# Attention times V: probabilities as the stationary operand, so that results come out with queries on partitions

## The chip, the cores and the metric

The kernel runs on one core of a Trainium2 chip. The metric is device time in microseconds (us), as the median of several executions. Engines are named as the profile names them: PE is the tensor engine, which multiplies matrices (PEld is its loading of weights, the stationary operand), ACT is ScalarE, which does the exponentials, DVE is VectorE, and SP issues the DMAs.

## The reference

A batch of 32 sequences, 512 positions, 8 heads of 64. For each sequence:

```
q, k, v = split(x_b @ w_qkv)                      # per head: [len, 64]
scores  = (q @ k.T) / sqrt(64)
attn    = exp(scores - max) / sum
out_b   = attn @ v                                # rows beyond len stay zero
```

## The kernel before

The kernel works in float16 with float32 sums, over all 512 positions, and masks by length. Per batch it transposes x (tiles `pxt`, `xT`), projects to q, k (`pq`, `qkT`) and v (`pv`, `v_aug`), computes scores with keys on partitions (`psc`), takes the exponential on ACT (`ep`), and multiplies by V. V carries one more column with the key mask, so the sum of the probabilities (the denominator) comes out of the same product. A compiler orders the instructions of all engines from this source.

Scores and exponentials (not touched by the change). The two heads of a pair use different halves of the array's rows:

```python
            for kt in range(NT):                               # 4 key tiles
                psc = ps_s.tile([P, 2, MAXS], FP32, tag="pssc")    # pool of 2
                for par in range(2):
                    rq = 64 * par
                    nc.tensor.matmul(psc[:, par, :],
                        qkT[rq : rq + 64, NC + i, kt * P : (kt + 1) * P],
                        qkT[rq : rq + 64, i, :], start=True, stop=True)
                nc.scalar.activation(out=ep[:, :, kt, :], in_=psc, func=AF.Exp, scale=scale)
```

The product with V. V is stationary, 512 queries stream, and the result has 65 head columns on partitions and queries along the row:

```python
                pav = ps_a.tile([P, MAXS], FP32, tag="psa")        # pool of 4
                for kt in range(NT):
                    nc.tensor.matmul(pav[0 : HD + 1, :], v_aug[:, kt, h, :],
                        ep[:, par, kt, :], start=(kt == 0), stop=(kt == NT - 1))
                nc.vector.tensor_copy(out=avout[0 : HD + 1, h, :], in_=pav[0 : HD + 1, :])
```

A separate output stage, one batch later, turns it round again with 32 PE transposes (`pot`), and normalises:

```python
        for qt in range(NT):
            pot = ps_a.tile([P, NH, HD + 2], F16, tag="psa")
            for h in range(NH):
                nc.tensor.transpose(pot[:, h, 0 : HD + 1],
                    avout[0 : HD + 1, h, qt * P : (qt + 1) * P], ...)
            # den8 = pot[:, :, HD] + qbig;  rcp8 = 1 / den8
            # out_nat[:, qt, :] = pot[:, :, 0:HD] * rcp8        (8 heads at once)
```

`qbig` is 1e30 for queries beyond the length, so those rows become zero.

The softmax here doesn't subtract the row's maximum and nothing guards it: scores larger than these inputs give would overflow.

## Time and profile before

The median is 948.5 us.

| | before |
|---|---|
| time, median of 4 | 948.5 us (946.9 to 950.4) |
| PE, DVE, ACT busy in the span | 94%, 63%, 58% |
| mean granted PE clock | 0.982 |
| one batch, mean of 20 in the middle of the trace | 28.44 us |

The first lines of the page give busy time, share and number of instructions of each engine; the chain that ended last follows the waits back from the end:

```profile
PE 891.2 (94%) x5120; PEld 363.4 (38%) x5120; DVE 592.6 (63%) x1094; ACT 547.5 (58%) x645; POOL 1.1 (0%) x8
...
PE 83%; ACT 10%; DVE 3%; issue 2%; DMA 1%; POOLq 0%; ACTq 0%; POOL 0%
```

They say "bound by PE". The groups of instructions (line, engine, operation, output <- input, shapes, count; then busy us, mean ns of one, and idle time before it with what ended it) show what the change will remove:

```profile
L180 ACT ACTIVATE ep<-psc 128x1024 f16<-128x1024 f32 x512 | 484.1, 1072 | 355.1 <-PE psc L173 355.1
L197 DVE CAST avout<-pav 65x512 f16<-65x512 f32 x256 | 172.9, 686 | 243.5 <-PE pav L190 243.5
L190 PE MATMUL pav<-ep,v_aug 128*65 128x512 f16 x1024 | 297.0, 388 | 0.0
...
L219 PE MATMUL pot<-ident_f_95,avout 65*128 65x65 f16 x1024 | 45.9, 194 | 2.8 <-DVE out_nat L232 1.4
```

The timeline of one batch (start and length in us, engine, line, what, count, and in brackets the idle time before) shows two stages and a tail:

```profile
301.72 0.60 PE L173 MATMUL psc<-qkT 64*128 64x512 f16 x3
302.14 12.02 ACT L180 ACTIVATE ep<-psc 128x1024 f16<-128x1024 f32 x13 [8.92 <-PE psc L173]
...
310.63 0.39 PE L173 MATMUL psc<-qkT 64*128 64x512 f16 x2
310.95 0.62 PE L190 MATMUL pav<-ep,v_aug 128*65 128x512 f16 x2
311.50 0.39 PE L173 MATMUL psc<-qkT 64*128 64x512 f16 x2
...
312.70 2.10 PE L190 MATMUL pav<-ep,v_aug 128*65 128x512 f16 x8
314.64 0.65 PE L219 MATMUL pot<-ident_f_95,avout 65*128 65x65 f16 x16
...
316.38 1.94 ACT L180 ACTIVATE ep<-psc 128x1024 f16<-128x1024 f32 x2 [2.21 <-PE psc L173]
...
319.70 1.03 PE L128 MATMUL pq<-xT,w_r 128*128 128x512 f16 x4
```

Read it so. ACT had been idle for 8.92 us, while PE did projections; then it does 13 exponentials in a row, 0.91 us apart. In most steps of this row PE does a pair of score matmuls and two products with V. In the tail the last eight products (2.10 us) and the output transposes go by, ACT is idle for 2.21 us, and the next projections (`pq`) start at 319.70. In a pair of score matmuls the second starts 3 to 6 ns after the first: they run side by side.

### The profile page before, as it was taken

How to read it: one execution, taken by the hardware profiler on the slowest of the kernel's cores; microseconds unless marked ns; L12 is line 12 of the kernel's file. 1: busy time of each engine (PE TensorE's matmuls, PEld its weight loads, DVE VectorE, ACT ScalarE, POOL GpSimd, SP SyncE). 2: the span in 40 equal slices, each digit the busy share in tenths (PEclk: the TensorE clock that was granted, in tenths of full speed). 3: DMA queues.
4: the chain of work that ended last, by engine and by line, in shares of the span. 5: the costliest groups of instructions: out<-in, count | busy, mean ns of one | idle time of the engine just before them, and what ended most of it. 6: DMA issues, size and time to landing. Idle time of an engine off the chain costs nothing.

```text
span 945.1 us, 12346 instructions
## 1 busy us (share of the span) xinstructions
PE 891.2 (94%) x5120; PEld 363.4 (38%) x5120; DVE 592.6 (63%) x1094; ACT 547.5 (58%) x645; POOL 1.1 (0%) x8
## 2 busy tenths in 40 slices
PE   2999999999999999999999999999999999999995
PEld 1433434433334433334433334433334433344332
DVE  2745667756667665567756667665566656666555
ACT  3177555576565567455576565567554575645764
POOL 0000000000000000000000000000000000000000
PEclk9899999999999999999999999999999999999997
DMA  9410222220222220222220222220122110111102
GB/s 330 159 45 1 89 89 89 90 72 31 76 90 89 89 89 23 68 90 89 90 72 32 76 89 90 89 82 25 72 90 89 45 45 1 45 45 45 45 26 108
DMA packets 34426, 71.05 MB, mean 75 GB/s; under 512 B 1090, under 2 KB 1090, under 8 KB 34370
## 3 DMA queue, kind: packets, MB, share of 16 engines
q1 hardware_dynamic: 34370, 70.26, 21.2%
q8 instruction: 40, 0.66, 0.3%
q14 instruction: 16, 0.13, 0.0%
HBM read 36.70 MB, written 33.55 MB: 74 GB/s over the span
## 4 chain that ended last, share of the span: by engine, by line
PE 83%; ACT 10%; DVE 3%; issue 2%; DMA 1%; POOLq 0%; ACTq 0%; POOL 0%
PE pav L190 25%; PE pq L128 23%; PE psc L173 18%; PE pv L142 12%; ACT ep L180 8%; PE pxt L118 3%; DVE avout L197 2%; PE pot L219 2%; ACT xT L121 2%; DMA w_f<-in_w_qkv_dram 1%; DVE out_nat L232 0%; ACT w_r L74 0%; POOLq L277 0%; ACTq L180 0%; DVE iota_f L86 0%
## 5 line engine op out<-in xcount | busy, mean ns | idle before, releaser
L180 ACT ACTIVATE ep<-psc 128x1024 f16<-128x1024 f32 x512 | 484.1, 1072 | 355.1 <-PE psc L173 355.1
L197 DVE CAST avout<-pav 65x512 f16<-65x512 f32 x256 | 172.9, 686 | 243.5 <-PE pav L190 243.5
L190 PE MATMUL pav<-ep,v_aug 128*65 128x512 f16 x1024 | 297.0, 388 | 0.0
L128 PE MATMUL pq<-xT,w_r 128*128 128x512 f16 x1024 | 239.5, 388 | 7.3 <-ACT w_r L74 7.2
L173 PE MATMUL psc<-qkT 64*128 64x512 f16 x1024 | 215.5, 385 | 17.0 <-ACT ep L180 13.1
L135 DVE CAST qkT<-pq 128x512 f16<-128x512 f32 x256 | 171.2, 689 | 58.9 <-PE pq L128 57.2
L128 PEld LDWEIGHTS <-w_r 128*128 128x128 f16 x1024 | 98.3, 100 | 128.6 <-issue 16.6
L190 PEld LDWEIGHTS <-v_aug 128*65 128x65 f16 x1024 | 84.2, 110 | 125.7 <-issue 100.1
L173 PEld LDWEIGHTS <-qkT 64*128 64x128 f16 x1024 | 60.5, 93 | 180.3 <-issue 170.9
L142 PE MATMUL pv<-w_r,xT 128*128 128x512 f16 x512 | 115.7, 379 | 0.0
L149 DVE TENSOR_SCALAR v_aug<-pv,kmask 128x512 f16<-128x512 f32 x128 | 96.4, 753 | 16.0 <-PE pv L142 5.5
L121 ACT COPY xT<-pxt 128x512 f16<-128x512 f16 x128 | 70.6, 603 | 22.6 <-PE pxt L118 22.0
L142 PEld LDWEIGHTS <-xT 128*128 128x128 f16 x512 | 50.1, 98 | 60.4
L219 PE MATMUL pot<-ident_f_95,avout 65*128 65x65 f16 x1024 | 45.9, 194 | 2.8 <-DVE out_nat L232 1.4
L219 PEld LDWEIGHTS <-avout 65*128 65x128 f16 x1024 | 38.9, 98 | 19.6 <-issue 7.8
L118 PE MATMUL pxt<-ident_f_95,x_129 128*128 128x128 f16 x16 | 1.9, 308 | 11.7 <-DVE ident_f_95 L67 11.7
L74 ACT CAST w_r<-w_f 128x1536 f16<-128x1536 f32 x4 | 5.8, 1488 | 5.3 <-DMA w_f<-in_w_qkv_dram 5.3
L154 DVE CAST v_aug<-kmask 128x32 f16<-128x32 f32 x32 | 7.4, 230 | 0.0
L118 PEld LDWEIGHTS <-x_129 128*128 128x128 f16 x16 | 1.7, 142 | 11.6 <-DVE x_129 L112 7.4
L112 DVE CAST x_129<-x_nat 128x2048 f16<-128x2048 f32 x1 | 1.2, 1227 | 6.1 <-DMA x_nat<-in_x_dram 6.1
L89 DVE TENSOR_TENSOR kmask<-iota_f,len_f 128x128 f32<-128x128 f32 x1 | 0.3, 292 | 5.1 <-POOL len_f L81 5.1
L86 DVE CAST iota_f<-iota_i 128x4 f32<-128x4 int32 x1 | 0.2, 246 | 3.8 <-POOL iota_i L84 3.8
(490 smaller groups left out, 262.4 us busy)
## 6 DMA issues: line engine op xcount, KB each, us to landing
x_nat<-in_x_dram SPq DMA_DIRECT2D x32, 1024.0 KB, 6.5
out_dram<-out_nat SPq DMA_DIRECT2D x32, 1024.0 KB, 4.9
w_f<-in_w_qkv_dram SPq DMA_DIRECT2D x4, 768.0 KB, 8.9
len_84<-in_lengths_dram SPq DMA_DIRECT2D x1, 0.2 KB
```

Source lines behind the costliest of these rows:

```text
L118: nc.tensor.transpose(pxt[:, t, :], x16[:, t, c * P : (c + 1) * P], ident_f16)
L121: nc.scalar.copy(out=xT[:, c, :], in_=pxt.rearrange("p t q -> p (t q)"))
L128: nc.tensor.matmul(pq, w_r[:, c, m * P : (m + 1) * P], xT[:, c, :], start=(c == 0), stop=(c == NC - 1),)
L135: nc.vector.tensor_copy(out=qkT[:, m, :], in_=pq)
L142: nc.tensor.matmul(pv, xT[:, c, t * P : (t + 1) * P], w_r[:, c, 2 * D : 3 * D], start=(c == 0), stop=(c == NC - 1),)
L149: nc.vector.tensor_scalar_mul(v_aug[:, t, :, 0:HD], pv.rearrange("p (h d) -> p h d", d=HD), kmask[:, t, b : b + 1],)
L154: nc.vector.tensor_copy(out=v_aug[:, :, :, HD], in_=kmask[:, :, b].unsqueeze(2).broadcast_to([P, NT, NH]),)
L173: nc.tensor.matmul(psc[:, par, :], qkT[rq : rq + 64, NC + i, kt * P : (kt + 1) * P], qkT[rq : rq + 64, i, :], start=True, stop=True,)
L180: nc.scalar.activation(out=ep[:, :, kt, :], in_=psc, func=AF.Exp, scale=scale)
L190: nc.tensor.matmul(pav[0 : HD + 1, :], v_aug[:, kt, h, :], ep[:, par, kt, :], start=(kt == 0), stop=(kt == NT - 1),)
L197: nc.vector.tensor_copy(out=avout[0 : HD + 1, h, :], in_=pav[0 : HD + 1, :])
L219: nc.tensor.transpose(pot[:, h, 0 : HD + 1], avout[0 : HD + 1, h, qt * P : (qt + 1) * P], ident_f16[0 : HD + 1, 0 : HD + 1],)
```

## The change

Swap the operands of the product. The probabilities of 128 queries are stationary, V with its ones column (65 columns) streams, and the result has queries on partitions, as the output needs it. The output transposes and the eviction to `avout` go; normalisation follows at once, for two heads and 128 queries at a time.

```diff
-            for par in range(2):
-                h = 2 * i + par
-                pav = ps_a.tile([P, MAXS], FP32, tag="psa")
-                for kt in range(NT):
-                    nc.tensor.matmul(pav[0 : HD + 1, :], v_aug[:, kt, h, :],
-                        ep[:, par, kt, :], start=(kt == 0), stop=(kt == NT - 1))
-                nc.vector.tensor_copy(out=avout[0 : HD + 1, h, :], in_=pav[0 : HD + 1, :])
+            for qt in range(NT):
+                pav = ps_a.tile([P, 2, HD + 1], FP32, tag="psa")
+                for par in range(2):
+                    for kt in range(NT):
+                        nc.tensor.matmul(pav[:, par, :],
+                            ep[:, par, kt, qt * P : (qt + 1) * P],
+                            v_aug[:, kt, 2 * i + par, :],
+                            start=(kt == 0), stop=(kt == NT - 1))
+                # den2 = pav[:, :, HD] + qbig;  rcp2 = 1 / den2
+                # out_nat[:, qt, i * P : (i + 1) * P] = pav[:, :, 0:HD] * rcp2
...
-    def stage_out(b):            # 32 transposes per batch, normalisation of 8 heads
...
-    for i in range(B + 2):
+    for i in range(B + 1):
```

Cuts are marked with dots; calls are drawn together. 1024 large products become 4096 small ones, and 1024 transposes go.

More of the change, by code (lines that the diff above doesn't have):

```diff
@@ L105 @@
     vaug_t = [None] * B
-    avout_t = [None] * B
     def stage_qkv(b):
@@ L161, in stage_attn @@
         v_aug = vaug_t[b]
-        avout = bav.tile([P, NH, MAXS], F16, tag="avout")
-        avout_t[b] = avout
+        out_nat = bo.tile([P, NT, D], FP32, tag="out_nat")
         etp = [None] * (NH // 2)
@@ L185, in emit_av @@
             ep = etp[i]
-            for par in range(2):
-                h = 2 * i + par
-                pav = ps_a.tile([P, MAXS], FP32, tag="psa")
-                for kt in range(NT):
-                    nc.tensor.matmul(
-                        pav[0 : HD + 1, :],
-                        v_aug[:, kt, h, :],
-                        ep[:, par, kt, :],
-                        start=(kt == 0),
-                        stop=(kt == NT - 1),
-                    )
-                nc.vector.tensor_copy(
-                    out=avout[0 : HD + 1, h, :], in_=pav[0 : HD + 1, :]
+            for qt in range(NT):
+                pav = ps_a.tile([P, 2, HD + 1], FP32, tag="psa")
+                for par in range(2):
+                    for kt in range(NT):
+                        nc.tensor.matmul(
+                            pav[:, par, :],
+                            ep[:, par, kt, qt * P : (qt + 1) * P],
+                            v_aug[:, kt, 2 * i + par, :],
+                            start=(kt == 0),
+                            stop=(kt == NT - 1),
+                        )
+                den2 = sml.tile([P, 2], FP32, tag="den2")
+                nc.vector.tensor_scalar(
+                    out=den2,
+                    in0=pav[:, :, HD],
+                    scalar1=qbig[:, qt, b : b + 1],
+                    scalar2=None,
+                    op0=ALU.add,
+                )
+                rcp2 = sml.tile([P, 2], FP32, tag="rcp2")
+                nc.vector.reciprocal(out=rcp2, in_=den2)
+                nc.vector.tensor_tensor(
+                    out=out_nat[:, qt, i * P : (i + 1) * P].rearrange(
+                        "p (h d) -> p h d", d=HD
+                    ),
+                    in0=pav[:, :, 0:HD],
+                    in1=rcp2.unsqueeze(2).broadcast_to([P, 2, HD]),
+                    op=ALU.mult,
                 )
@@ L208, in stage_attn @@
         emit_av(3)
-    def stage_out(b):
-        avout = avout_t[b]
-        avout_t[b] = None
-        out_nat = bo.tile([P, NT, D], FP32, tag="out_nat")
-        for qt in range(NT):
-            den8 = sml.tile([P, NH], FP32, tag="den8")
-            rcp8 = sml.tile([P, NH], FP32, tag="rcp8")
-            pot = ps_a.tile([P, NH, HD + 2], F16, tag="psa")
-            for h in range(NH):
-                nc.tensor.transpose(
-                    pot[:, h, 0 : HD + 1],
-                    avout[0 : HD + 1, h, qt * P : (qt + 1) * P],
-                    ident_f16[0 : HD + 1, 0 : HD + 1],
-                )
-            nc.vector.tensor_scalar(
-                out=den8,
-                in0=pot[:, :, HD],
-                scalar1=qbig[:, qt, b : b + 1],
-                scalar2=None,
-                op0=ALU.add,
-            )
-            nc.vector.reciprocal(out=rcp8, in_=den8)
-            nc.vector.tensor_tensor(
-                out=out_nat[:, qt, :].rearrange("p (h d) -> p h d", d=HD),
-                in0=pot[:, :, 0:HD],
-                in1=rcp8.unsqueeze(2).broadcast_to([P, NH, HD]),
-                op=ALU.mult,
-            )
         nc.sync.dma_start(out=out[b].rearrange("(t p) d -> p t d", p=P), in_=out_nat)
-    for i in range(B + 2):
+    for i in range(B + 1):
         if i < B:
@@ L244 @@
             stage_attn(i - 1)
-        if i >= 2:
-            stage_out(i - 2)
 _INS = ['x', 'w_qkv', 'lengths', 'n_heads']
```

## The prediction

> What bounds it now. The page's busy shares (PE 94%, DVE 63%, ACT 58%) mislead: in the timeline two stages alternate, about 28.2 us per batch (between ends of V projections; mostly 27.6 and 28.9).
> (1) Projection: 48 matmuls of 512 columns, 216 ns start to start, 10.4 us, PE-bound; ACT idle for about 9 us (the waits give ACT 355 us idle, ended by the score matmuls).
> (2) Attention: 12 or 13 exponentials back to back. A row of 13 lasts 12.02 us; less one duration (1.07) over 12 is 0.91 us each. In such a step PE does one score pair and two probability-times-V matmuls (0.32 + 0.56 us) and is full too: a balance of ACT and PE.
> (3) A tail of about 6 us: the last 8 to 10 probability-times-V matmuls (2.1 to 2.5 us), 32 output transposes with score matmuls between, x transposes and copies. ACT is idle 2.2 to 2.7 us there.
>
> Removed: 1024 matmuls of 512 columns (216 to 242 ns apart, about 230 us of PE), 1024 output transposes (16 in 0.65 us, the last 0.19: 31 ns each, about 35 us), 256 evictions of 65x512 (172.9 us of DVE), 128 sets of wide output operations.
> Added: 4096 matmuls with 65 moving columns, each with its own 128-column weights. The output transposes have that shape but for 65 rows instead of 128: 31 ns. The Trainium skill (TensorE: Matmul & The Clock Gate, LDWEIGHTS) says load time goes by columns, not rows; nothing in this trace shows it at 128 rows. Estimate 4096 x 31 ns = 127 us. So PE sheds about 140 us. DVE: 512 sets of add, reciprocal, multiply: pitches 0.13 and 0.12 us, and a multiply over 128 instead of 512 columns, about 0.20 us (its 0.60 us pitch less 384 columns at the 0.96 GHz of the skill's VectorE: DVE Perf Modes). 0.45 us a set, 0.75 if each waits for the one before: 230 to 380 us, against about 310 removed. DVE stays under 80%.
>
> Critical path. The compiled order puts 14 exponentials (12 of this batch, two of the next) in one row behind the projection, with 8 to 12 small matmuls between score pairs: 0.25 to 0.37 us plus 0.32 us per 0.91 us step, so PE has slack and ACT alone paces: 0.4 + 14 x 0.91 = 13.1 us. Four x copies follow (0.47 us each); projections start under them. So 13.1, about 2 us until the last copy, some 9.4 us for the projections left then: 24.5 to 25.3 us per batch instead of 28.2. The row hardly shrinks; the gain is the PE tail (2 us of large matmuls, 1.5 to 2 us of transposes) and ACT's idle in it. 30 periods save about 100 us; at the end there is no separate output stage: 5 to 8 us more.
>
> Predicted 835 us, range 805 to 872. Faster by over 2%: 0.94; within 2%: 0.04; slower: 0.02.
>
> To check: exponentials 0.91 us apart in rows of about 14; small matmuls about 30 ns apart; ACT busy about 65%; PE busy 75-85%; the chain of waits shows ACT's exponential far above its 8%; V projections end 24.5-25.5 us apart.
>
> What would make it wrong: small accumulating matmuls at 55-65 ns (the step exceeds 0.91 us, about 870 in all); PE waiting for PSUM tiles that the four-buffer pool returns only after DVE's three dependent operations; a lower granted clock because PE is less dense.

## More of the kernel before

On PE, no step of the row with two products is shorter than 0.872 us: 3 ns between the two score matmuls, 316 to the first product, 241 to the second, 312 to the next score. Steps in which PE waits for ACT take 0.914 to 0.917 us: there the last distance is 350 to 355 ns. On ACT, two exponentials are never less than 0.904 us apart, and that is their usual distance. So ACT is the slower of the two in the row, but only by 0.03 us.

## The result

| | before | after |
|---|---|---|
| time, median of 4 | 948.5 us | 867.9 us (867.3 to 868.3) |
| PE, DVE, ACT busy | 94%, 63%, 58% | 89%, 65%, 64% |
| mean granted PE clock | 0.982 | 0.994 |
| one batch, mean of 20 | 28.44 us | 26.02 us |

The ratio is 0.9147, with a 95% interval of 0.9128 to 0.9167. Here and below a ratio is that of the record, from fast runs of the same rounds, so not quite the ratio of the medians quoted. Results are correct. The changed kernel is 80.6 us faster; 113 had been forecast.

The same lines of the page for the changed kernel:

```profile
PE 771.8 (89%) x7168; PEld 410.7 (47%) x7168; DVE 562.0 (65%) x1990; ACT 549.9 (64%) x645; POOL 1.1 (0%) x8
...
PE 53%; ACT 41%; issue 3%; DMA 1%; POOLq 0%; DVE 0%; ACTq 0%; POOL 0%
...
L178 ACT ACTIVATE ep<-psc 128x1024 f16<-128x1024 f32 x512 | 482.1, 1068 | 281.6 <-PE psc L171 280.2
L171 PE MATMUL psc<-qkT 64*128 64x512 f16 x1024 | 230.0, 381 | 57.5 <-ACT ep L178 36.8
...
L188 PE MATMUL pav<-v_aug,ep 128*128 128x65 f16 x4096 | 206.2, 195 | 11.1 <-ACT ep L178 11.1
```

In the chain ACT went from 10% to 41%. PE now waits for ACT: 36.8 us before score matmuls, by the waits, where it was 13.1 us. Most of the small products start 29 to 30 ns apart (median 30; the others in a group 33 to 40), though each is recorded for 195 ns. This is part of why PE's busy share hardly fell, beside the shorter span: records of pipelined matmuls overlap and cover gaps. The Trainium skill (Perfetto Trace Analysis, "Identifying the Most-Contended Engine") says that matmul busy share is not a good measure of the distance to the roofline, and here it is seen: 89% busy, while the order experiment below has PE waiting a quarter of a microsecond in each step under such a record.

One batch of the changed kernel:

```profile
310.35 0.61 PE L171 MATMUL psc<-qkT 64*128 64x512 f16 x4
310.84 11.10 ACT L178 ACTIVATE ep<-psc 128x1024 f16<-128x1024 f32 x12 [8.64 <-PE psc L171]
...
318.33 0.39 PE L171 MATMUL psc<-qkT 64*128 64x512 f16 x2 [0.18 <-ACT ep L178]
318.66 0.53 PE L188 MATMUL pav<-v_aug,ep 128*128 128x65 f16 x12
319.25 0.39 PE L171 MATMUL psc<-qkT 64*128 64x512 f16 x2
...
321.86 0.39 PE L171 MATMUL psc<-qkT 64*128 64x512 f16 x1
322.18 0.79 PE L188 MATMUL pav<-v_aug,ep 128*128 128x65 f16 x20
322.34 2.01 ACT L178 ACTIVATE ep<-psc 128x1024 f16<-128x1024 f32 x2 [0.40 <-PE psc L171]
...
324.25 2.12 ACT L120 COPY xT<-pxt 128x512 f16<-128x512 f16 x4
...
325.48 0.38 PE L127 MATMUL pq<-xT,w_r 128*128 128x512 f16 x1
```

Compare one typical period of each kind, measured from its first score matmul behind the V projection (before has two kinds, which alternate):

| us from the start of the period | before | after |
|---|---|---|
| last product with V starts | 12.28 / 12.71 | 12.42 |
| first x transpose starts | 14.55 / 16.04 | 13.37 |
| first projection starts | 16.52 / 17.98 | 15.13 |
| period ends | 27.57 / 28.86 | 26.01 |

The stage with the products is hardly shorter. Of the 2.2 us that a batch gained (the mean of the two kinds against the one), 2.0 lie between the last product and the first projection: 4.24 and 5.27 us before, 2.71 after.

In the span as a whole, 945.1 us before and 865.4 after, the last matmul of the second V projection starts at 47.2 and 46.5 us, that of the last V projection 854.6 and 784.2 us later, and what follows takes 43.2 and 34.7 us. So 70.4 us come from the 30 periods, 8.5 from the end of the program, which has no output stage of its own any more, and 0.7 from the start.

### The profile page after: what moved, and what is told of

Read it like the earlier page. It is cut to its first block, busy times and chain, and to the rows that moved or that the text cites. A ratio compares the mean times of both kernels' runs of the same rounds, so it can differ in the third digit from the quotient of the medians.

```text
span 865.5 us, 17340 instructions
## 1 busy us (share of the span) xinstructions
PE 771.8 (89%) x7168; PEld 410.7 (47%) x7168; DVE 562.0 (65%) x1990; ACT 549.9 (64%) x645; POOL 1.1 (0%) x8
## 4 chain that ended last, share of the span: by engine, by line
PE 53%; ACT 41%; issue 3%; DMA 1%; POOLq 0%; DVE 0%; ACTq 0%; POOL 0%
ACT ep L178 40%; PE pq L127 26%; PE pv L141 13%; PE psc L171 8%; PE pxt L117 4%; PE pav L188 2%; DMA w_f<-in_w_qkv_dram 1%; ACT w_r L74 0%; POOLq L259 0%; ACT xT L120 0%; ACTq L178 0%; ACTq L259 0%; DVE out_nat L205 0%; DVE iota_f L86 0%; DVE ident_f_95 L67 0%
## 5 line engine op out<-in xcount | busy, mean ns | idle before, releaser
L171 PE MATMUL psc<-qkT 64*128 64x512 f16 x1024 | 230.0, 381 | 57.5 <-ACT ep L178 36.8
L127 PE MATMUL pq<-xT,w_r 128*128 128x512 f16 x1024 | 235.9, 384 | 6.4 <-ACT w_r L74 6.4
L188 PE MATMUL pav<-v_aug,ep 128*128 128x65 f16 x4096 | 206.2, 195 | 11.1 <-ACT ep L178 11.1
L134 DVE CAST qkT<-pq 128x512 f16<-128x512 f32 x256 | 173.9, 690 | 53.7 <-PE pq L127 53.5
L188 PEld LDWEIGHTS <-ep 128*128 128x128 f16 x4096 | 152.3, 97 | 116.2 <-issue 93.7
L171 PEld LDWEIGHTS <-qkT 64*128 64x128 f16 x1024 | 81.7, 93 | 96.5 <-issue 55.4
L120 ACT COPY xT<-pxt 128x512 f16<-128x512 f16 x128 | 67.6, 591 | 20.8 <-PE pxt L117 20.7
L111 DVE CAST x_129<-x_nat 128x2048 f16<-128x2048 f32 x1 | 1.2, 1227 | 6.0 <-DMA x_nat<-in_x_dram 6.0
L111 DVE CAST x_6203<-x_nat 128x2048 f16<-128x2048 f32 x1 | 1.2, 1228 | 1.6 <-PE pxt L117 1.6
L111 DVE CAST x_8193<-x_nat 128x2048 f16<-128x2048 f32 x1 | 1.2, 1228 | 1.3 <-PE pxt L117 1.3
```

What stands on the lines that cost most here:

```text
L111: nc.vector.tensor_copy(out=x16, in_=x_nat)
L120: nc.scalar.copy(out=xT[:, c, :], in_=pxt.rearrange("p t q -> p (t q)"))
L127: nc.tensor.matmul(pq, w_r[:, c, m * P : (m + 1) * P], xT[:, c, :], start=(c == 0), stop=(c == NC - 1),)
L134: nc.vector.tensor_copy(out=qkT[:, m, :], in_=pq)
L171: nc.tensor.matmul(psc[:, par, :], qkT[rq : rq + 64, NC + i, kt * P : (kt + 1) * P], qkT[rq : rq + 64, i, :], start=True, stop=True,)
L188: nc.tensor.matmul(pav[:, par, :], ep[:, par, kt, qt * P : (qt + 1) * P], v_aug[:, kt, 2 * i + par, :], start=(kt == 0), stop=(kt == NT - 1),)
```

## The experiments

The theory at this point: the row of exponentials is paced by ACT, so the cheaper products turn into waits of PE; the gain is the tail, where the output stage stood. The rival: PE's work bounds the kernel, and each microsecond of PE saved or added counts. Twelve kernels were run; each was timed in three rounds beside the kernel before, whose medians were 946.6 to 948.8 us. The runs were spread over two chips (`before_no_output_stage`, the two `twice` runs in an order fixed by hand and `even_steps_three_ops` ran on the second); the kernel before took 948.8 us in the rounds of the four other hand-ordered runs and 948.3 on the second chip, so the differences below can be compared across them.

| run | median us | ratio to before |
|---|---|---|
| changed kernel | 867.9 | 0.9147 |
| before_1of8_transposes (wrong result) | 922.1 | 0.9725 |
| before_no_output_stage (wrong result) | 896.3 | 0.9464 |
| after_products_twice | 1011.7 | 1.0677 |
| after_half_exp (wrong result) | 792.7 | 0.8364 |
| before_half_exp (wrong result) | 884.4 | 0.9332 |
| rows_before | 902.4 | 0.9522 |
| rows_after | 880.8 | 0.9288 |
| rows_after_twice | 889.6 | 0.9386 |
| even_steps_before | 870.9 | 0.9183 |
| even_steps_after | 744.6 | 0.7852 |
| even_steps_after_twice | 859.0 | 0.9066 |
| even_steps_three_ops | 744.6 | 0.7857 |

### The output transposes alone

```diff
-            for h in range(NH):
+            for h in range(1):          # DVE reads this one head eight times
                 nc.tensor.transpose(pot[:, h, 0 : HD + 1], ...)
```

> Wrong result on purpose: the kernel before with one output transpose per query tile instead of eight (896 fewer); the vector engine still does all its output operations. Theory: the transposes stand in the tail, where PE is the pace, so nearly all of 896 x 31 ns = 28 us comes off: 915 to 925 us. Rival: they are hidden under other waits: 940 us or more.

Measured 922.1 us, 24.5 us under the 946.6 of its rounds. 896 transposes at 31 ns are 28 us: most of their PE time seems to have been on the critical path, as the theory has it. But the run isn't clean. Its periods no longer alternate (27.46 us; nearly every batch has 11 large products in a block behind the row where the kernel before has 8 or 10), so the compiler moved other work too, and it has three stretches at half clock where the kernel before has five (see the end). The 30 periods got 23.3 us shorter; about 2 us of that are the clock. By proportion all 1024 transposes would be worth about 24 us in the periods, an estimate.

### The whole output stage

```diff
-    def stage_out(b): ...              # transposes, normalisation
+    def stage_out(b):                  # stores a constant tile
+        nc.sync.dma_start(out=out[b].rearrange("(t p) d -> p t d", p=P), in_=out_const)
```

> Wrong result on purpose: the kernel before without its output stage (no output transposes, no normalisation; the store sends a constant tile), large products and their evictions kept; the compiler chooses the order. Theory: the changed kernel's gain in the given order came from the output stage's going, not from the cheaper products, which only made PE idle in a row paced by ACT; so this is about as fast as the changed kernel: 850 to 885 us. Rival: the products' 100 us of PE work count: 910 us or more.

Measured 896.3 us: between the two expectations, so neither holds as written. Without the stage, the compiler chose another order: all 16 exponentials now stand in the row, none beside the tail or the projections. The last product starts at 15.52 us instead of 12.3 to 12.7, and the projections follow soon, at 16.69. The stage gave 52 us (about 7 of them the clock: this run has no stretch at half clock among its batches), but part of its tail had been used by ACT for exponentials. Its period is 27.15 us, and the changed kernel's is 26.01. This run does not isolate a cause; it shows that removing work also moves other work.

### Products twice, and exponentials halved, with the compiler's order

```diff
-                    for kt in range(NT):
+                    for kt2 in range(2 * NT):       # same sums twice: still correct
+                        kt = kt2 % NT
```

> The changed kernel with every small probability-times-V product done twice into the same sums (numerator and denominator both double, so the result stays right): 4096 more matmuls at 30 ns, 3.9 us more PE work per batch. Theory: ACT paces the attention row, one step of PE becomes 0.32 + 16 x 0.03 + about 0.1 = 0.9 us, still under 0.912, so only the last 20 products and uneven steps show: 1 to 2 us per batch, 900 to 930 us. Rival: PE work bounds the kernel: plus 122 us, about 990 us.

Measured 1011.7 us, more than even the rival expected. But the build had another order: no products stood at the very head of the row, 99 of them in one block at its end, and no exponential beside the projections. The mean granted clock fell to 0.941. The test does not tell the theories apart; it was repeated below with the order fixed.

```diff
-                ep = epool.tile([P, 2, NT, MAXS], F16, tag="et")
+                ep = epool.tile([P, 2, NT, MAXS // 2], F16, tag="et")
...
-                    out=ep[:, :, kt, :], in_=psc, func=AF.Exp, scale=scale
+                    out=ep[:, :, kt, :], in_=psc[:, :, 0 : MAXS // 2], func=AF.Exp, scale=scale
```

In both kernels the products read the 256 columns twice, so that PE's work stays; that part of the edit is left out here.

> Wrong result on purpose: the changed kernel with each exponential over 256 of the 512 queries (ACT about 0.48 instead of 0.91 us a step), all PE work kept. Theory: ACT paces the row, so the step falls to PE's 0.65 to 0.7 us and the tail's two exponentials shrink: 3 to 4 us per batch, 745 to 775 us. Rival: PE bounds it: over 850 us.

> Wrong result on purpose: the same halving of the exponentials in the kernel before, all PE work kept (the moving operand reads the 256 columns twice). Theory: PE is as full as ACT there (0.87 to 0.88 us per step), so only some 0.5 us of the row and up to 1 us of the tail come off: 900 to 925 us. If ACT alone paced it, about as much as in the changed kernel would come off: below 850 us. If PE alone: 940 us or more.

Measured 792.7 us from the changed kernel (75 us less) and 884.4 us from the kernel before (62 us less). Both outcomes miss their ranges. Halving ACT's work helped the kernel before almost as much, which suggests that ACT held it too, in the row or the tail. But here too both builds had a new order, so how much of this is ACT's work and how much the order is not shown.

### The order fixed by hand: two stages, or spread evenly

From here on PE, ACT and DVE issue in the order of the source. One step is a pair of scores with its exponential, and one group of products five steps behind. In `rows` all projections of the next batch stand in one bunch after step 5 of each 16; in `even_steps` one projection tile, or one set of four x transposes, stands in each step. Each was built with the products of the changed kernel and with those of the kernel before (with its transposes, spread over the steps). x is transposed one batch ahead. In the expectations below, "excursion" is the time that PE loses by going to a score pair and back. Normalisation takes two DVE operations instead of three: a reciprocal, and one multiplication by it and by a 0/1 mask.

```diff
     for s in range(16 * B):
         b, u = s // 16, s % 16
         scores(b, u // 4, u % 4)
-        if u == 5:                                    # rows
-            unit_pxt(b + 2, 0..3); unit_pq(b + 1, 0..7); unit_pv(b + 1, 0..3)
+        if u % 4 == 3: unit_pxt(b + 2, u // 4)        # even_steps
+        else:          one of unit_pq(b + 1, 0..7), unit_pv(b + 1, 0..3)
         av_step(s - 5)
```

> The changed form of the products with the order of PE, ACT and DVE fixed by hand: 16 score pairs in a row, each followed by one group of 8 small products, then all projections of the next batch in one bunch (as in the changed kernel, two stages alternate). x transposes one batch ahead; normalisation in two vector operations. Theory (ACT paces the row at 0.91 us, PE alone paces the bunch of 10.4 us): 14 x 0.91 + 10.4 + 0.9 + 0.3 = 24.3 us per batch, 815 to 845 us in all. If PE paces everything the row is 16 x 0.77 us and it falls below 800.

> The same order by hand with the products in the form of the kernel before (large products, one head every second step, 32 output transposes spread over the row). Theory: a step costs PE 0.52 us for the scores and its excursion plus 2 x 0.228 for the products = 0.98 us, more than ACT's 0.91, so PE paces the row too: about 27.3 us per batch, 905 to 940 us. So the change of form is worth about 95 us in this order.

> As rows_after, but the 12 projection tiles and 4 x transposes are spread, one after each score pair, so ACT and PE work at the same time all through. Theory: now PE is the pace with its sum: 16 x (0.52 + 0.25) + 10.4 + 0.9 = 23.6 us per batch by the excursion costs read from the changed kernel; 760 to 805 us, 20 to 60 us faster than rows_after. Rival: if the order of the stages doesn't matter, within 10 us of rows_after.

> As rows_before, but projections spread as in even_steps_after. Theory: PE paces both orders in this form, so spreading brings little: within 20 us of rows_before, 890 to 935 us; and the change of form is worth 120 us or more in this order, against 80 between the two given kernels. Rival: spreading brings as much here as in the other form.

| | products as before | products as after | difference |
|---|---|---|---|
| rows | 902.4 us | 880.8 us | 21.6 us |
| even steps | 870.9 us | 744.6 us | 126.3 us |

The same change is worth 22 us in one order and 126 in the other. (About 10 us of the gap come from something else: in `rows_after` the last x transpose and the first projection start 1.14 us apart, in `rows_before` 0.81, because of the x copies on ACT; 0.33 us in each of 30 periods is an estimate of what that costs.) In `even_steps` PE has work at all times, so what the change takes from PE comes off the time. Its periods are 26.09 and 22.08 us: 4.01 us a batch, 128 us in all, is what the change really saves PE.

All four expectations missed. `rows_before` came out just below its range, at 902.4 us, and the change of form is worth 22 us in this order, not 95. `rows_after` was to take 815 to 845 us: it had been assumed that two exponentials run beside the bunch, but the x copies on ACT stand behind them, and the projections wait for the copies' tiles. So 16 exponentials follow each other in 14.77 us, and PE's bunch comes on top. `even_steps_before` gained 31 us from spreading, where at most 20 were expected: PE was not quite the pace in `rows_before`, whose chain of waits has ACT at 31%. And `even_steps_after` was faster than its 760 to 805 us: the excursion to a score pair had been put at 0.52 us, and measured 0.44 (319 ns to the next full-array matmul, 125 from the last product).

Why the row swallows the products is seen in the timelines. `rows_after`:

```profile
426.57 14.77 ACT L173 ACTIVATE ep<-psc 128x1024 f16<-128x1024 f32 x16 [9.71 <-PE psc L166]
...
430.40 0.39 PE L166 MATMUL psc<-qkT 64*128 64x512 f16 x2 [0.17 <-ACT ep L173]
430.72 0.42 PE L188 MATMUL pav<-vaug,ep 128*128 128x65 f16 x8
431.31 0.39 PE L166 MATMUL psc<-qkT 64*128 64x512 f16 x2 [0.18 <-ACT ep L173]
```

A step is 0.91 us, the pace of ACT. PE has done its eight products early and waits: from the start of the last product to the next score it takes 367 ns (median), against 125 ns in `even_steps_after`, where nothing holds it. That is about 0.24 us of slack a step. `even_steps_after`:

```profile
401.89 0.39 PE L166 MATMUL psc<-qkT 64*128 64x512 f16 x2
402.22 1.04 PE L129 MATMUL pq<-xT,w_r 128*128 128x512 f16 x4
403.09 0.40 PE L188 MATMUL pav<-vaug,ep 128*128 128x65 f16 x8
403.43 0.39 PE L166 MATMUL psc<-qkT 64*128 64x512 f16 x2
...
403.86 1.02 ACT L173 ACTIVATE ep<-psc 128x1024 f16<-128x1024 f32 x1 [0.51 <-PE psc L166]
```

Now ACT waits for PE (0.51 us in this step), and PE goes on without a break. The Trainium skill says that a kernel whose most-contended engine changes over time may gain from interleaving these regimes (Perfetto Trace Analysis, "Optimization Strategy"). This agrees, with 880.8 to 744.6 us.

### Products twice, order fixed

> rows_after (880.8 us, order fixed by hand) with every small product done twice into the same sums: 128 more matmuls of 30 ns per batch, 3.9 us of PE work, nothing else changed and no instruction moved. In rows_after PE waits about 0.24 us for ACT in each step of the row (last product to next score 367 ns, against 125 ns where nothing holds it). Theory: 8 x 30 ns fill that wait and cost nothing in the row; only the two steps by the projection bunch and uneven ones show: 0 to 1 us per batch, 880 to 910 us. Rival (PE work bounds): plus 123 us, about 1004 us.

> The same doubling in even_steps_after (744.6 us), where PE is busy 96% and never waits long. Theory: here the same 3.9 us per batch are on the critical path: plus 105 to 125 us, 850 to 870 us.

The edit is that of `after_products_twice`, and the order of the others stays as it is. 4096 more matmuls, about 123 us of PE work, cost 8.9 us in `rows` (880.8 to 889.6) and 114.4 us in `even_steps` (744.6 to 859.0). This is the test that tells the theories apart, and in this order the row's theory holds: where the stages alternate, the work of the products is almost free. The step of `rows_after_twice` has 16 products and the same length:

```profile
430.83 0.39 PE L166 MATMUL psc<-qkT 64*128 64x512 f16 x2
431.15 0.66 PE L189 MATMUL pav<-vaug,ep 128*128 128x65 f16 x16
431.74 0.39 PE L166 MATMUL psc<-qkT 64*128 64x512 f16 x2
```

The waits tell the same; first `rows_after` (who <- whom: us in total, times, longest):

```profile
PE psc L166 <- ACT ep L173: 75.3, 417, 1.4
```

then `rows_after_twice`:

```profile
PE psc L166 <- ACT ep L173: 2.6, 4, 1.4
```

### Three vector operations or two

```diff
-        # rcp2 = 1 / pav[:, :, HD];  out = pav * mask * rcp2
+        # den2 = pav[:, :, HD] + qbig;  rcp2 = 1 / den2;  out = pav * rcp2
```

> even_steps_after with the normalisation as in the changed kernel (add, reciprocal, multiply: 512 more vector operations), order fixed by hand. Theory: DVE has room (72% busy), so 0 to 20 us slower: 745 to 765 us; what made 744.6 us is the order of the stages. If DVE's chain paced it, 16 x 0.25 us per batch = 128 us would come on top: over 850.

Measured 744.6 us, the same as with two. DVE is then busy 82% instead of 72%, and it costs nothing. So DVE's chain of three dependent operations costs nothing in this order, and the 744.6 us don't come from leaving one out. In the changed kernel's own order this was not tested.

## Why the prediction was right or wrong

The time held: 867.9 us lies within 805 to 872, near its upper edge, and 71% of the expected gain came (80.6 of 113 us). That it fell inside is partly luck: the text gives "about 870" only for products 55 to 65 ns apart, which did not happen (30 ns), and the time came near 870 by another way, a longer batch. Point by point:

- **Two alternating stages; ACT alone paces the row after the change.** Right. The chain shows ACT's exponential at 40%, and the doubling in the `rows` order shows that PE has room in such a step.
- **"ACT and PE" in balance before.** Right, within 0.03 us: PE's step with two products took 0.872 us where it waited for nothing, ACT's 0.904. The change raised PE's slack to about 0.24 us (in `rows_after` a step of PE is 3 + 319 + 225 + 125 ns = 0.67 us, and the step lasts 0.91). So "the row hardly shrinks" was right.
- **Small products at about 31 ns.** Right: mostly 29 to 30 ns at 128 rows, as the transposes at 65 rows. The skill's statement (LDWEIGHTS) that columns and not rows count for the load agrees as far as rows go: the loads of 128 columns are recorded for 98 ns at 65 rows and 97 ns at 128. That columns count, no run here shows.
- **PE sheds about 140 us.** About right: 128 us where PE is the pace throughout. In the compiler's order only 70 us came off the periods, part of it from other causes.
- **DVE stays under 80%; its multiply about 0.20 us.** Right: 65%, and 198 ns between two multiplies that follow each other. The 0.20 us was an estimate from the clock in the skill's page.
- **No output stage at the end: 5 to 8 us.** Measured 8.5 us.
- **24.5 to 25.3 us per batch.** This is the step that was mis-sized: 26.01 us. Its first term, 14 exponentials in one row and the first x copy at 13.1 us, measured 13.90: after 12 exponentials there is a break, because the next batch's first pair of scores stands on PE behind products that wait for the fifteenth exponential, and three products stand between its two halves. ACT idles 0.40 us at that place. Its second term, "about 2 us until the last copy", measured 2.12. Its third term, 9.4 us of projections left after the last copy, measured 9.99: when the last copy ended, three projection matmuls had started, the third 0.03 us before, and not four or five, since a score matmul stands behind the first one. 0.80 + 0.12 + 0.59 us are the 1.51 us from 24.5 to 26.01. Against the middle of the forecast range, 24.9, it is 1.1 us a batch, and 30 periods of that are the 33 us by which 835 was too low.
- **PE busy 75 to 85%.** Wrong: 89%. The records of small matmuls last 195 ns each and overlap.
- **A lower granted clock, as a danger.** The reverse: 0.982 rose to 0.994 (see below).

What stays open: of the 70 us in the periods, the transposes account for about 24, by the estimate above, and the clock for about 7. The remaining 39 us or so, 1.3 us a batch, lie mostly in the tail, between shorter last products, shorter holding of tiles by DVE, and a different order of exponentials there. No run separates these, since each such edit made the compiler choose another order; for the same reason the 24 us are not clean either.

## What to carry to other kernels

Before counting what an engine saves, find which engine paces each stage, from the distance between the starts of its instructions; work saved on the other engine turns into waiting until the stages are interleaved. Here the same change was worth 22 us with the stages in turn and 126 us with them spread, and the spread order with the new products (744.6 us, correct) beats both kernels. When a scheduler orders the instructions, fix the order before using an edit as an experiment: doubling the same products cost 144 us with the order left free, and 9 or 114 us with it fixed.

## What the Trainium skill lacked or had wrong

- TensorEngine Tiling (Array Packing), "Key Properties", says that changing the tiling mode drains the engine, without a size. Sizes: from the second half-array score matmul to a full-array matmul 315 to 320 ns instead of 216 for 512 columns, and from a 65-column product to a score pair 125 ns instead of 30. No run tells how much of that is the change of mode.
- TensorE: Matmul & The Clock Gate, "Back-to-back issue gap", gives about 81 ns for 128 columns and 131 ns for 512 as the sustained spacing of weight load and matmul pairs. Here every matmul has its own load, and the usual spacings are 55 to 56 ns and 216 ns; for 65 columns 29 to 30 ns. These are the values of the page's formula for an isolated gap, N / 2.4 + 2.5 ns.
- The same page warns of idle gaps of more than about 3 us as what halves the clock. In the kernel before, five later windows of 3.4 us ran at half clock, and each came behind a stretch in which PE had 3.0 of 3.5 us of recorded work. In the windows of the trace (PE busy is the first number behind the length, the clock the third from the end):

```profile
371.50:375.00 3.50, 3.00 (x37) 1.48 (x34) 3.50 (x13) 2.19 (x3) 0.00 (x0) 1.00 0.00 0
375.00:378.50 3.50, 3.50 (x19) 1.55 (x17) 2.12 (x4) 3.45 (x6) 0.00 (x0) 0.52 0.53 201
```

  The stretch holds output and x transposes and scores. The page's "Part 4: PE-mode transpose" says that transposes do not count as busy in the same way, which would fit, and the changed kernel, and the one without output stage, had no such window between the first 40 us and the end of the work. But the record also speaks against it: `after_products_twice`, without output transposes, has such a window in nearly every batch, `before_1of8_transposes` has three, and `even_steps_before`, with all 1024, has none. Nor do 3.0 us of work suffice for it: 315.17 to 318.67 us holds the same work, and the clock stayed full. So the cause stays open. The five periods concerned are 1.35 us longer than the others, 6.8 us in all.
- Perfetto Trace Analysis tells that the matmul row is a poor measure, but not by how much it hides: 195 ns recorded for small matmuls that start 30 ns apart, and 0.24 us of waiting a step while PE shows 85% busy (`rows_after`). The reason it gives, that pipelined instructions look smaller in the trace, is not what these records show: they are longer than the spacing.
